# Two-bank PSUM tiles and row-tiled attention, with the modulation products moved to three other engines

## The chip, the cores and the metric

One core of one Trainium2 chip runs the whole program. The metric is the time on the device in microseconds (us), and the median of several runs is what counts. The engines are TensorE (PE; its weight loads are shown apart as PEld), VectorE (DVE), ScalarE (ACT), GpSimd (POOL) and SyncE (SP), which issues the loads.

## What is computed

The reference is one step of a two-layer trunk over 384 tokens: 128 context tokens ("prompt") and 256 latent tokens, of width 1024. Each layer has a mixer (three token mixers A, B, C and three gates from one wide input projection) and a squared-ReLU MLP. Before each of them the tokens are normalised and modulated by vectors computed from a conditioning vector, one for the context and one for the latents. Cut to what matters here:

```python
def trunk_layer(x, cond, l, w, ctx):
    mod = silu(cond) @ w_mod[l] + b_mod[l]              # 1024 x 6144, for two conds
    sh1, sc1, g1, sh2, sc2, g2 = split(mod, 6)
    h = rms_norm(x, norm1[l]) * (1 + sc1) + sh1
    x = x + g1 * mixer(h)
    h = rms_norm(x, norm2[l]) * (1 + sc2) + sh2
    return x + g2 * (square(relu(h @ w_fc1[l])) @ w_fc2[l])

# mixer: z = h @ w_in; A = gated linear attention (4 heads, low-rank decay gates alf @ w_a2_f, alb @ w_a2_b)
# B, C = softmax attention, 8 heads of 64: prompt against prompt, latents against local + context keys
#   p = softmax(q k^T / 8 + bias);  out = p v
# out = (sigmoid(ga) * A w_pa + sigmoid(gb) * B w_pb + sigmoid(gc) * C w_pc) @ w_o
```

## The kernel before

The large products run through "units": 512 KB of float32 weights are loaded into one of three `raw` buffers, ACT rounds them to float32r (`whi`), DVE takes the remainder (`wlo`, L172), and PE forms hi x hi, hi x lo and lo x hi (24 matmuls of 384 columns, named `mmf`, or 18 of 512, named `mmt`). `run` issues loads six units ahead, the cut three ahead, then the unit's matmuls; between units it advances up to three background tasks by one `yield` each. The tasks are the attention: `attn_prompt`, `attn_pair`, `gla_pre`, `gla_main`. The Tile framework then sets the order on every engine, and each engine works through its list in order.

PSUM has eight banks: four for `mmf`/`mmt`, three single-bank buffers with the tag `bx` for everything of the attention, one with the tag `md`. In `attn_pair` a pair of heads is handled in two tiles t of 128 latents. For each, two tiles `ps` (one bank a head) take the scores of 384 keys (L706), and a DVE instruction adds the mask and finds the maximum (L711). These products are plain float32 with 64 rows of contraction: one head lies in rows 0 to 63, the other in rows 64 to 127. The trace counts two passes for each float32 product. `attn_prompt` treats the two halves of the heads one after the other. `gla_pre` multiplies the gates' low-rank part with `wa2` in four products `pz` (L761) that hold only 32 rows.

The modulation vectors are made in blocks of 512 columns, each in four units of two channel blocks. Of layer 0, blocks 0 to 3 are made at the start by `mod_first`. Blocks 4 to 6 use `mod_pe`: 8 products with `sT` into four column tiles of one bank (L212). The other 17 use `mod_dve`: DVE multiplies and adds in SBUF for both conditions (L243, L245), and at the end PE transposes eight 128x128 pieces into `md` (L252), which DVE reduces (L253). `weave` puts the units between the others at places that the constants give: in layer 0's mixer `mod_pe` from unit 6 and `mod_dve` from unit 28, in layer 1's mixer `mod_dve` from unit 30, the rest in the MLPs. In the mixers these units use the same three `raw` buffers as the weights.

Of the kernel before, what the change touches and what calls it, by code (L numbers as in the profile page):

```python
# [42 lines left out]
def trunk_kernel(ctx: ExitStack, tc: tile.TileContext, A: dict):  # L43
# [8 lines left out]
    pbx = ctx.enter_context(tc.tile_pool(name="pbx", bufs=3, space=PSUM))  # L52
    pmd = ctx.enter_context(tc.tile_pool(name="pmd", bufs=1, space=PSUM))
# [54 lines left out]
    ones = pers.tile([128, 256], F32, name="ones")  # L108
# [92 lines left out]
    def mod_pe(l, cc, acc_alloc, raw_alloc=None):  # L201
        w = A["w_mod"][l].rearrange("(k p) n -> p k n", p=128)
        out = []
        for u in range(4):
# [20 lines left out]
            out.append(un)
        return out

    def mod_dve(l, cc, alloc, raw_alloc=None):
        """512 adaLN columns: products summed over the channel blocks on the vector engine, over the partitions by PE."""
        w = A["w_mod"][l].rearrange("(k p) n -> p k n", p=128)  # L230
        out = []
        for u in range(4):
            def comp(un, u=u):
# [3 lines left out]
                for i in range(2):  # L237
                    kt = 2 * u + i
                    wv = un.raw[:, i * 512:(i + 1) * 512]
                    for c in range(2):  # L240
                        s_ = sT[:, kt, c:c + 1]
                        if kt == 0:
                            ts(acc[c], wv, s_, ALU.mult)  # L243
                        else:
                            stt(acc[c], wv, s_, acc[c], ALU.mult, ALU.add)  # L245
                if u == 3:
                    c4 = slice(4 * cc, 4 * cc + 4)
                    m = modcol[l][:, c4, :]
                    for c in range(2):
                        pc = pmd.tile([128, 4, 128], F32, tag="md", name="md")  # L250
                        for i in range(4):
                            nc.tensor.transpose(pc[:, i, :], acc[c][:, i * 128:(i + 1) * 128], ident)  # L252
                        nc.vector.tensor_reduce(out=m[:, :, c], in_=pc, axis=AX.X, op=ALU.add)  # L253
                    tt(m, m, last(P(f"bm{l}")[:, c4], 2), ALU.add)
# [251 lines left out]

# [869 lines left out]
```

## Time and profile before

| | |
|---|---|
| median of 3 runs (lowest, highest) | 1435.33 us (1434.57, 1438.09) |
| profiled execution, its own span | 1433.7 us, 24064 instructions |
| PE busy | 1406.7 us (98%), 9386 matmul passes |
| PEld busy | 1274.5 us (89%) |
| DVE busy | 1008.5 us (70%) |
| ACT busy | 694.5 us (48%) |
| POOL busy | 29.5 us (2%) |
| granted TensorE clock, mean | 0.999 |

Busy time of an engine is the union of its instructions' spans. A matmul's span ends when its results have landed, so the spans of neighbours overlap, and a PE that waits for less than such a tail does not look idle. The pitch of PE is read from the starts of neighbouring matmuls instead. The profiled execution spans 1.6 us less than the median of the runs.

### The profile page before, as it was taken

Reading aid. Unit: us, or ns where it says so; the run is one execution under the profiler, and the core shown is the slowest. Engines: PE = TensorE matmul, PEld = TensorE weight load, DVE = VectorE, ACT = ScalarE, POOL = GpSimd, SP = SyncE. Lnnn points to the kernel's source line nnn. Section 1 sums busy time; section 2 is a strip of 40 time slices with the busy share of each in tenths; the row PEclk is TensorE's granted clock in tenths of the full one; section 3 lists DMA queues with packets and bytes.
Section 4 is the critical chain, followed back from the end, with each engine's and each line's share of the span. In section 5 each row is a group of like instructions: output and inputs, shape, how many; then the busy total and the mean of one; then the engine's idle time right before and its main releaser. Section 6 shows DMA issues by size and latency. Waiting matters only on the chain.

```text
span 1433.7 us, 24064 instructions
## 1 busy us (share of the span) xinstructions
PE 1406.7 (98%) x9386; PEld 1274.5 (89%) x9386; DVE 1008.5 (70%) x2032; ACT 694.5 (48%) x1260; POOL 29.5 (2%) x55
## 2 busy tenths in 40 slices
PE   6999999999999999999999999999999999999998
PEld 5876667889999999999998677689999999999998
DVE  5577466977767888877777875779986688553332
ACT  3456357643335666633335565565433556663221
POOL 0000000010000000000000000000200000000000
PEclk9999999999999999999999999999999999999999
DMA  9842533464654556556654325434555465343441
GB/s 282 232 128 79 149 99 96 134 184 135 173 177 148 179 183 183 178 193 195 191 159 125 89 59 141 127 96 112 171 155 176 147 194 159 118 130 121 137 141 61
DMA packets 191762, 212.70 MB, mean 148 GB/s; under 512 B 22656, under 2 KB 152832, under 8 KB 191648
## 3 DMA queue, kind: packets, MB, share of 16 engines
q1 hardware_dynamic: 189760, 206.18, 49.1%
q0 software_dynamic: 1600, 4.59, 0.8%
q8 instruction: 74, 1.21, 0.4%
q14 instruction: 40, 0.33, 0.1%
q10 hardware_dynamic: 288, 0.39, 0.1%
HBM read 206.15 MB, written 4.98 MB: 147 GB/s over the span
## 4 chain that ended last, share of the span: by engine, by line
PE 81%; DVE 10%; DMA 3%; ACT 2%; issue 2%; SPq 0%; DVEq 0%; ACTq 0%
PE mmf L76 57%; PE mmt L76 13%; DVE wlo L64 3%; PE ps L76 3%; PE po L76 2%; DMA raw<-in_w_in_dram 2%; PE pp L732 2%; DVE macc L67 1%; PE md L76 1%; ACT whi L57 1%; PE md L252 1%; DVE dd L64 1%; DMA raw<-in_w_mod_dram 1%; DVE K L64 1%; DVE Q L64 1%
## 5 line engine op out<-in xcount | busy, mean ns | idle before, releaser
L64 DVE TENSOR_TENSOR wlo<-raw,whi 128x1024 fp32r<-128x1024 f32 (+1 forms) x280 | 338.9, 1210 | 216.9 <-ACT whi L57 216.0
L57 ACT ACTIVATE whi<-raw 128x1024 fp32r<-128x1024 f32 (+1 forms) x280 | 293.9, 1050 | 389.7 <-PE mmf L76 283.0
L76 PE MATMUL mmf<-hh,whi 128*128 128x386 f32 (+1 forms) x960 | 328.3, 344 | 0.5 <-ACT whi L57 0.5
L76 PE MATMUL mmf<-hh,wlo 128*128 128x386 f32 (+1 forms) x960 | 327.0, 341 | 0.0
L76 PE MATMUL mmf<-hl,whi 128*128 128x386 f32 (+1 forms) x960 | 326.7, 340 | 0.0
L76 PEld LDWEIGHTS mmf<-hh,whi 128*128 128x128 f32 x960 | 181.1, 189 | 7.5 <-issue 5.4
L76 PEld LDWEIGHTS mmf<-hl,whi 128*128 128x128 f32 x960 | 181.6, 189 | 1.1 <-issue 0.9
L76 PEld LDWEIGHTS mmf<-hh,wlo 128*128 128x128 f32 x960 | 181.5, 189 | 0.5 <-DVE wlo L64 0.2
L76 PE MATMUL mmf<-h2h,wlo 128*128 128x384 f32 x512 | 173.7, 339 | 0.0
L76 PE MATMUL mmf<-h2h,whi 128*128 128x384 f32 x512 | 173.7, 339 | 0.0
L76 PE MATMUL mmf<-h2l,whi 128*128 128x384 f32 x512 | 173.4, 339 | 0.0
L76 PE MATMUL mmt<-whi,hh 128*128 128x512 f32 (+1 forms) x336 | 131.2, 392 | 0.0
L76 PE MATMUL mmt<-wlo,hh 128*128 128x512 f32 (+1 forms) x336 | 130.5, 388 | 0.0
L76 PE MATMUL mmt<-whi,hl 128*128 128x512 f32 (+1 forms) x336 | 129.0, 384 | 0.0
L67 DVE SCALAR_TENSOR_TENSOR macc<-mraw,sT,macc 128x512 f32<-128x512 f32 x140 | 99.1, 749 | 5.2 <-DMA mraw<-in_w_mod_dram 5.2
L76 PEld LDWEIGHTS mmf<-h2h,whi 128*128 128x128 f32 x512 | 96.1, 188 | 0.0
L76 PEld LDWEIGHTS mmf<-h2l,whi 128*128 128x128 f32 x512 | 96.1, 188 | 0.0
L76 PEld LDWEIGHTS mmf<-h2h,wlo 128*128 128x128 f32 x512 | 96.1, 188 | 0.0
L57 ACT ACTIVATE rl<-rl,sw 128x128 f32<-128x128 f32 (+1 forms) x128 | 51.5, 447 | 60.7 <-DVE rl L64 60.5
L76 PEld LDWEIGHTS mmt<-whi,hh 128*128 128x128 f32 x336 | 63.1, 188 | 19.6 <-issue 7.9
L67 DVE SCALAR_TENSOR_TENSOR macc<-raw,sT,macc 128x512 f32<-128x512 f32 x98 | 70.2, 753 | 10.9 <-DMA raw<-in_w_mod_dram 10.9
L76 PEld LDWEIGHTS mmt<-wlo,hh 128*128 128x128 f32 x336 | 63.3, 188 | 15.3 <-issue 5.6
(248 smaller groups left out, 2002.3 us busy)
## 6 DMA issues: line engine op xcount, KB each, us to landing
raw<-in_w_fc_dram SPq DMA_DIRECT2D x128, 512.0 KB, 3.6
raw<-in_w_in_dram SPq DMA_DIRECT2D x96, 512.0 KB, 3.8
mraw<-in_w_mod_dram SPq DMA_DIRECT2D x56, 512.0 KB, 4.7
raw<-in_w_mod_dram SPq DMA_DIRECT2D x40, 512.0 KB, 3.9
raw<-in_w_o_dram SPq DMA_DIRECT2D x16, 512.0 KB, 3.5
raw<-in_w_in_dram SPq DMA_DIRECT2D x24, 256.0 KB, 5.0
raw<-in_w_pb_dram SPq DMA_DIRECT2D x16, 256.0 KB, 4.3
raw<-in_w_pc_dram SPq DMA_DIRECT2D x8, 512.0 KB, 3.5
```

What stands on the lines that cost most here:

```text
L57: return nc.scalar.activation(out=out, in_=in_, func=func, **kw)
L64: nc.vector.tensor_tensor(out=out, in0=a, in1=b, op=op)
L67: nc.vector.scalar_tensor_tensor(out=out, in0=a, scalar=s, in1=b, op0=op0, op1=op1)
L76: nc.tensor.matmul(out, lhsT, rhs, start=start, stop=stop)
L252: nc.tensor.transpose(pc[:, i, :], acc[c][:, i * 128:(i + 1) * 128], ident)
L732: nc.tensor.transpose(pp[:, s, :], sc[:, t, c * 128:(c + 1) * 128], ident)
```

## The change

PSUM: the three `bx` buffers and the `md` buffer become two buffers of two banks each (`bx2`); single-bank users take the first bank of one. Scores: the two heads' products alternate in pieces of 256 and 128 columns, each head in a bank of its own; a `yield` stands after each t, and a pair of mixer C starts when the pair before it has its scores. Prompt: all eight heads in one pass of the task, with the two halves' last products alternating. Gates: `al` is repeated four times so that the four `pz` products lie in four row tiles of 32. Modulation: both `mod_pe` and `mod_dve` give way to `mod_units`: the context's sums stay on DVE, the latents' products go to ACT (in place, in the loaded buffer) and their sums to POOL; at the end DVE transposes 32x32 blocks and reduces, and PE sums over partitions with a 128x32 matrix `fold`, four products of 8 columns. Layer 0's mixer then weaves all of blocks 4 to 9 from unit 5, every 1.7 units; layer 1's mixer blocks 6 to 9 from unit 12, every 2.2.

```diff
-    pbx = ctx.enter_context(tc.tile_pool(name="pbx", bufs=3, space=PSUM))
-    pmd = ctx.enter_context(tc.tile_pool(name="pmd", bufs=1, space=PSUM))
+    pbx = ctx.enter_context(tc.tile_pool(name="pbx", bufs=2, space=PSUM))
...
+    def bx2(name):
+        return pbx.tile([128, 2, 512], F32, tag="bx", name=name)
+
+    def bank(t, b, shape):
+        n = int(np.prod(shape[1:]))
+        v = t[0:shape[0], b, 0:n]
+        return v if len(shape) == 2 else v.rearrange("p (a b) -> p a b", b=shape[2])
+
+    def bx(shape, name):
+        return bank(bx2(name), 0, shape)
...
+    fold = pers.tile([128, 32], F32, name="fold")
+    nc.vector.tensor_reduce(out=fold, in_=ident.rearrange("p (b i) -> p i b", i=32), axis=AX.X, op=ALU.add)
...
-    def mod_pe(l, cc, acc_alloc, raw_alloc=None):
...
-    def mod_dve(l, cc, alloc, raw_alloc=None):
+    def mod_units(l, cc, alloc, tmp, raw_alloc=None):
...
                     wv = un.raw[:, i * 512:(i + 1) * 512]
+                    if kt == 0:
+                        ts(acc[0], wv, sT[:, 0, 0:1], ALU.mult)
+                        act(acc[1], wv, AF.Copy, scale=sT[:, 0, 1:2])
+                    else:
+                        stt(acc[0], wv, sT[:, kt, 0:1], acc[0], ALU.mult, ALU.add)
+                        act(wv, wv, AF.Copy, scale=sT[:, kt, 1:2])
+                        nc.gpsimd.tensor_tensor(out=acc[1], in0=wv, in1=acc[1], op=ALU.add)
+                if u == 3:
+                    part = small.tile([128, 32], F32, tag="part", name="part", bufs=2)
                     for c in range(2):
...
+                        tr = tmp()
+                        nc.vector.transpose(tr, acc[c])
+                        nc.vector.tensor_reduce(out=part[:, 16 * c:16 * c + 16], in_=tr.rearrange("p (b j) -> p b j", j=32),
+                                                axis=AX.X, op=ALU.add)
+                    pv = part.rearrange("p (c q a) -> p a q c", c=2, a=4)
+                    ps = bx([128, 4, 2], "md")
+                    for a in range(4):
+                        mm(ps[32 * a:32 * a + 32], fold, pv[:, a])
...
-                ps = [bx([128, T], "ps") for _ in range(2)]
+                ps = bx2("ps")
                 o = 256 - 128 * t
-                for r, p_ in zip(rows, ps):
-                    mm(p_, qT[r, j, 128 + 128 * t:256 + 128 * t], M["kTB"][r, 128:512] if m == "B" else M["kTC"][r, j, o:o + T])
+                for c0, n in ((0, 256), (256, 128)):
+                    for i, r in enumerate(rows):
+                        kk = M["kTB"][r, 128 + c0:128 + c0 + n] if m == "B" else M["kTC"][r, j, o + c0:o + c0 + n]
+                        mm(ps[:, i, c0:c0 + n], qT[r, j, 128 + 128 * t:256 + 128 * t], kk)
...
+            po = bx([128, 4, 128], "po")
+            for j in range(4):
+                for half, r in halves:
                     v = M["vB"][:, 0, r] if m == "B" else M["vC"][:, 0, (2 * j + half) * 64:(2 * j + half) * 64 + 64]
-                    mm(po[r, j, :], v, pT[:, j, :])
+                    mm(po[r, j, :], v, pTs[half][:, j * 128:(j + 1) * 128])
...
+            pz = [bx2("pz") for _ in range(2)]
+            for c0, n in ((0, 256), (256, 128)):
+                for i in range(4):
+                    r = slice(32 * i, 32 * i + 32)
+                    mm(pz[i // 2][:, i % 2, c0:c0 + n], wa2[r, :], alT[r, c0:c0 + n])
...
-MOD0, MODE0, MOD1, MODE1, MOD2, MODE2, MODS, MODM = 6, 2.5, 30, 2, 28, 2.4, 2, 2
+MOD0, MODE0, MOD1, MODE1, MODS, MODM = 5, 1.7, 12, 2.2, 2, 2
```

The first place is PE in layer 0's mixer where the scores of B's first three pairs stand (`ps`; `mmt` are the input projection's matmuls). Before:

```order
L76 MATMUL mmt_1215<-wlo_1011,hh_273 128x512
L76 MATMUL ps_1137<-kTB_105,qTB_107 128x384
L76 MATMUL ps_1138<-kTB_105,qTB_107 128x384
L76 MATMUL ps_1143<-kTB_105,qTB_107 128x384
L76 MATMUL ps_1144<-kTB_105,qTB_107 128x384
L76 MATMUL ps_1179<-kTB_105,qTB_107 128x384
L76 MATMUL ps_1180<-kTB_105,qTB_107 128x384
L76 MATMUL ps_1185<-kTB_105,qTB_107 128x384
L76 MATMUL ps_1186<-kTB_105,qTB_107 128x384
L76 MATMUL ps_1196<-kTB_105,qTB_107 128x384
L76 MATMUL ps_1197<-kTB_105,qTB_107 128x384
L76 MATMUL ps_1202<-kTB_105,qTB_107 128x384
```

On the same engine at the same place in the changed program:

```order
L75 MATMUL mmt_1257<-whi_1043,hh_272 128x512
L75 MATMUL ps_1121<-kTB_104,qTB_106 128x256 x2
L75 MATMUL ps_1121<-kTB_104,qTB_106 128x128 x2
L75 MATMUL ps_1132<-kTB_104,qTB_106 128x256 x2
L75 MATMUL ps_1132<-kTB_104,qTB_106 128x128 x2
L75 MATMUL mmt_1257<-wlo_1044,hh_272 128x512
L75 MATMUL mmt_1257<-whi_1043,hl_273 128x512
L75 MATMUL ps_1157<-kTB_104,qTB_106 128x256 x2
L75 MATMUL ps_1157<-kTB_104,qTB_106 128x128 x2
L75 MATMUL ps_1164<-kTB_104,qTB_106 128x256 x2
L75 MATMUL ps_1164<-kTB_104,qTB_106 128x128 x2
L75 MATMUL mmt_1243<-whi_1239,hh_272 128x512
```

Eleven scores in a row, each in a buffer of its own, have become groups of two buffers, two heads in each, with projection matmuls between them.

The second place is PE, also in layer 0's mixer, where a unit of the modulation stands (`md`). Before, one unit of `mod_pe`:

```order
L76 MATMUL mmt_1229<-whi_1010,hh_273 128x512
L76 MATMUL mmt_1229<-wlo_1011,hh_273 128x512
L76 MATMUL mmt_1229<-whi_1010,hl_274 128x512
L76 MATMUL md_1014<-raw_932,sT_85 32x512 x2
L76 MATMUL mmt_1215<-whi_1211,hh_273 128x512
L76 MATMUL mmt_1215<-wlo_1212,hh_273 128x512
```

In the changed program PE has only the end of a block, on the same engine and in the same stage:

```order
L75 MATMUL mmt_1593<-whi_1378,hl_273 128x512
L75 MATMUL mmt_1579<-whi_1547,hl_273 128x512
L622 MATMUL pq_1517<-ident_77,cq_1155 128x128 x4
L75 MATMUL md_1564<-part_1557,fold_84 32x8 x4
L75 MATMUL mmt_1586<-whi_1547,hh_272 128x512
L75 MATMUL mmt_1586<-wlo_1548,hh_272 128x512
```

Twelve units of two products of 512 columns and their transposes are gone there; four products of 8 columns stand once a block.

The third place is DVE early in layer 0's MLP, at the end of a modulation block (`rl`, `sw`, `h2l` belong to the MLP's activations). Before:

```order
L64 TENSOR_TENSOR rl_5161<-mmf_5103,nrb_4832 128x384
L64 TENSOR_TENSOR wlo_5173<-raw_5084,whi_5172 128x1024
L64 TENSOR_TENSOR h2l_4943<-rl_5140,h2h_4942 128x384
L64 TENSOR_TENSOR h2l_4943<-rl_5161,h2h_4942 128x384
L253 TENSOR_REDUCE modcol0_91<-md_5208 128x4
L64 TENSOR_TENSOR wlo_5224<-raw_5122,whi_5223 128x1024
L253 TENSOR_REDUCE modcol0_91<-md_5214 128x4
L71 TENSOR_SCALAR macc_5303<-mraw_5116,sT_85 128x512
L64 TENSOR_TENSOR modcol0_91<-modcol0_91,par_78 128x8
```

Changed, DVE at the same block's end (`macc_4957` is the sum that POOL adds up):

```order
L66 SCALAR_TENSOR_TENSOR macc_4956<-mraw_5063,sT_82,macc_4956 128x512 x2
L63 TENSOR_TENSOR wlo_4966<-raw_4894,whi_4965 128x1024
L1177 COPY sw_4978<-mmf_4866 128x2
L63 TENSOR_TENSOR rl_4977<-mmf_4866,nrb_4864 128x384
L1177 COPY sw_4993<-mmf_4873 128x2
L63 TENSOR_TENSOR rl_4992<-mmf_4873,nrb_4864 128x384
L1177 COPY sw_5008<-mmf_4880 128x2
L238 STREAM_TRANSPOSE mtr_5248<-macc_4956 128x512
L238 STREAM_TRANSPOSE mtr_5251<-macc_4957 128x512
L1177 COPY sw_5023<-mmf_4887 128x2
L239 TENSOR_REDUCE part_5247<-mtr_5248 128x16
L63 TENSOR_TENSOR h2l_4976<-rl_4977,h2h_4975 128x384
```

Where DVE took a finished transpose out of PSUM, it now transposes itself, and its second transpose reads what POOL has written.

## Rows read from the trace of the kernel before

**Rows 1.** The page's first part: busy us (share of the span) xinstructions.
```profile
PE 1406.7 (98%) x9386; PEld 1274.5 (89%) x9386; DVE 1008.5 (70%) x2032; ACT 694.5 (48%) x1260; POOL 29.5 (2%) x55
```

**Rows 2.** Windows: length, then PE, PEld, DVE, ACT, POOL busy, PEclk, DMA, GB/s.
```profile
75.00:350.00 275.00, 271.03 (x2117) 208.31 (x2116) 205.67 (x482) 149.74 (x313) 8.71 (x16) 0.99 0.45 125
465.00:758.00 293.00, 293.00 (x1687) 290.96 (x1686) 229.12 (x411) 138.54 (x229) 4.40 (x8) 1.00 0.59 180
830.00:1065.00 235.00, 230.84 (x1955) 190.75 (x1954) 191.06 (x403) 125.58 (x248) 9.60 (x14) 1.00 0.45 124
```

**Rows 3.** Instruction groups by form on PE: xcount | busy us, mean ns.
```profile
L76 PE MATMUL ps<-kTC,qTC 64*128 64x384 f32 x64 | 23.1, 533 | 0.7 <-ACT pT L57 0.7
...
L252 PE MATMUL md<-ident,macc 128*128 128x128 f32 x136 | 21.4, 280 | 0.6 <-DVE modcol L253 0.5
L76 PE MATMUL ps<-kTB,qTB 64*128 64x384 f32 x64 | 19.7, 535 | 0.2
L76 PE MATMUL md<-raw,sT 128*32 128x512 f32 x48 | 14.7, 605 | 0.0
...
L76 PE MATMUL pz<-alT,wa 32*128 32x384 f32 x16 | 7.0, 527 | 0.0
...
L76 PE MATMUL po<-pT,vB 128*64 128x128 f32 x32 | 4.4, 279 | 0.0
```

**Rows 4.** Timeline in layer 0's scores of B: start us, length us, engine, instruction.
```profile
104.65 6.45 PE L76 MATMUL ps<-kTB,qTB 64*128 64x384 f32 x22
...
106.67 0.61 DVE L711 CUSTOM_DVE_ANT_0 sc<-ps,swam,par 128x384 f32<-128x384 f32 x1
...
106.81 0.29 PEld L76 LDWEIGHTS ps<-kTB,qTB 64*128 64x128 f32 x2 [0.24 <-DVE mx L711]
```

**Rows 5.** Timeline of PE: products of two column tiles, then of two row tiles.
```profile
123.93 1.51 PE L76 MATMUL po<-pT,vB 128*64 128x256 f32 x12
...
163.12 1.16 PE L76 MATMUL sp<-kTC,qTC 64*128 64x128 f32 x16
```

**Rows 6.** Timeline of PE around one unit of the old PE modulation.
```profile
116.68 0.40 PE L76 MATMUL mmt<-wlo,hh 128*128 128x512 f32 x1
116.91 0.40 PE L76 MATMUL mmt<-whi,hl 128*128 128x512 f32 x1
117.23 1.05 PE L76 MATMUL md<-raw,sT 128*32 128x512 f32 x4
118.22 0.50 PE L76 MATMUL mmt<-whi,hh 128*128 128x512 f32 x1
118.55 0.39 PE L76 MATMUL mmt<-wlo,hh 128*128 128x512 f32 x1
```

**Rows 7.** Timeline of PE in layer 0's MLP, at the transposes of a block.
```profile
532.71 0.60 PE L252 MATMUL md<-ident,macc 128*128 128x128 f32 x4
533.06 0.42 PE L76 MATMUL mmf<-hh,whi 128*128 128x386 f32 x1
533.32 0.33 PE L76 MATMUL mmf<-hl,whi 128*128 128x386 f32 x1
533.49 0.34 PE L76 MATMUL mmf<-hh,wlo 128*128 128x386 f32 x1
```

**Rows 8.** Instruction groups by form on DVE and ACT: xcount | busy us, mean ns.
```profile
L67 DVE SCALAR_TENSOR_TENSOR macc<-mraw,sT,macc 128x512 f32<-128x512 f32 x140 | 99.1, 749 | 5.2 <-DMA mraw<-in_w_mod_dram 5.2
...
L253 DVE TENSOR_REDUCE modcol<-md 128x4 f32<-128x512 f32 x34 | 23.4, 687 | 18.1 <-PE md L252 18.1
...
L57 ACT ACTIVATE macc<-md 128x512 f32<-128x512 f32 x3 | 1.8, 601 | 6.0 <-PE md L76 6.0
```

**Rows 9.** POOL's groups by form, and its copies by tile (duration ns min/median/max).
```profile
L131 POOL MEMSET tb<- 128x640 f32 x2 | 1.2, 634 | 0.0
...
L828 POOL COPY As<-Ac x16: 334/696/1450, 287.8 to 1011.9; 32x192 f32<-32x192 f32 x16
```

**Rows 10.** DVE's sums by tile (min/median/max ns), while POOL copied at 1007 to 1011.
```profile
L67 DVE SCALAR_TENSOR_TENSOR macc<-raw,sT,macc x4: 824/826/852, 1007.5 to 1009.7; 128x512 f32<-128x512 f32 x4
```

More of the change, by code (lines that the diff above doesn't have):

```diff
@@ L239, in comp @@
                     wv = un.raw[:, i * 512:(i + 1) * 512]
-                    for c in range(2):
[L241 to L246, printed above, removed]
-                    c4 = slice(4 * cc, 4 * cc + 4)
[L248 to L254, printed above, removed]
+                    if kt == 0:
[7 more added lines that the diff above has]
+                    part = small.tile([128, 32], F32, tag="part", name="part", bufs=2)
+                    for c in range(2):
+                        tr = tmp()
[6 more added lines that the diff above has]
+                        mm(ps[32 * a:32 * a + 32], fold, pv[:, a])
+                    c4 = slice(4 * cc, 4 * cc + 4)
+                    tt(modcol[l][:, c4, :], ps, last(P(f"bm{l}")[:, c4], 2), ALU.add)
                     mod_done(l, cc)
@@ L505, in w25 @@
             return mt([128, 640], "w25", 4, name)
-        def bx(shape, name):
-            return pbx.tile(shape, F32, tag="bx", name=name)
         M["vB"] = mt([128, 4, 128], "vB", 1, "vB")
@@ new lines, in attn_prompt @@
+                    mm(sp[:, half, j * 128:(j + 1) * 128], qT[r, j, 0:128], kk)
+            s8 = sp.rearrange("p h (j k) -> p (h j) k", k=128)
+            mx = small.tile([128, 16], F32, tag="mx", name="mx", bufs=2)
+            nc.vector.tensor_reduce(out=mx[:, 0:8], in_=s8, axis=AX.X, op=ALU.max)
+            sk = P(f"sink{l}")
+            if m == "B":
+                tt(mx[:, 0:8], mx[:, 0:8], sk, ALU.max)
+            ts(mx[:, 8:16], mx[:, 0:8], -1.0, ALU.mult)
+            dn = small.tile([128, 16], F32, tag="dn", name="dn", bufs=2)
@@ new lines, in attn_prompt @@
+            prs = [t2("pr").rearrange("p (j k) -> p j k", j=4) for _ in range(2)]
+            for i in range(8):
+                act(prs[i // 4][:, i % 4, :], s8[:, i, :], AF.Exp, bias=mx[:, 8 + i:9 + i], accum_out=dn[:, i:i + 1])
+            if m == "B":
+                tt(dn[:, 8:16], sk, mx[:, 0:8], ALU.subtract)
+                act(dn[:, 8:16], dn[:, 8:16], AF.Exp)
+                tt(dn[:, 0:8], dn[:, 0:8], dn[:, 8:16], ALU.add)
+            yield
+            nc.vector.reciprocal(dn[:, 0:8], dn[:, 0:8])
@@ new lines, in attn_prompt @@
+            for half, r in halves:
+                tt(prs[half], prs[half], last(dn[:, 4 * half:4 * half + 4], 128), ALU.mult)
+            yield
+            pp = bx2("pp")
+            for i in range(8):
+                nc.tensor.transpose(pp[:, i // 4, (i % 4) * 128:(i % 4 + 1) * 128], prs[i // 4][:, i % 4, :], ident)
+            pTs = [t2("pT") for _ in range(2)]
+            for half, r in halves:
+                act(pTs[half], pp[:, half, :])
+            yield
+            po = bx([128, 4, 128], "po")
@@ L710, in attn_pair @@
                                    (consts["tb"][i][:, o:o + T], -3.0e38))
-                    nc.vector.tensor_tensor_reduce(out=scs[i][:, t, 0:T], in0=ps[i], in1=bias, scale=1.0, scalar=floor,
+                    nc.vector.tensor_tensor_reduce(out=scs[i][:, t, 0:T], in0=ps[:, i, 0:T], in1=bias, scale=1.0, scalar=floor,
                                                    op0=ALU.add, op1=ALU.max, accum_out=mxs[i][:, t:t + 1])
-            for half, (r, h, sc, mx) in enumerate(zip(rows, heads, scs, mxs)):
+                if t == 1:
+                    done.add(N(f"sc{m}{j}"))
+                yield
+            for h, sc, mx in zip(heads, scs, mxs):
                 dn = small.tile([128, 2], F32, tag="dn2", name="dn2")
-                yield
                 n = T
@@ L802, in products @@
                 s = t if s is None else s
-                ps = [bx([128, 2, 128], "pA") for _ in range(2)]
+                pa = bx2("pA")
+                ps = [bank(pa, hp, [128, 2, 128]) for hp in range(2)]
                 for g in range(2):
@@ L813, in blocks @@
             def blocks(Q, K, w, x):
-                ps = [bx([128, 6, w], "pA") for _ in range(2)]
+                pa = bx2("pA")
+                ps = [bank(pa, hp, [128, 6, w]) for hp in range(2)]
                 for i in range(6):
@@ L1009, in ev_cv @@
                 for j in range(4):
[L1010 removed]
+                    spawn(N(f"aC{j}"), after([N(f"ck{i}") for i in range(3)] + [N(f"scC{i}") for i in range(j)], attn_pair("C", j)))
                 spawn(N("gpre"), after([N("aBp")] + [N(f"aB{j}") for j in range(4)], gla_pre()))
@@ L1032, in comp @@
                             fps[c] = pmm.tile([128, T], F32, tag="mm", name="mmf")
+                        two = bx2("mmt")
                         for t in range(3):
-                            fps[4 + t] = bx([128, 512], "mmt")
+                            fps[4 + t] = two[:, t, :] if t < 2 else mdst["pair"][:, 0, :]
                     hh, hl = hs["hh"][:, kt, :T], hs["hl"][:, kt, :T]
```

147 lines of the change are left out of this document (48 added, 99 removed).

## Prediction

> **What bounds the kernel now.** I read the page's first part, then the windows of the stages, then single stretches of PE. PE is busy for 1406.7 of 1433.7 us [rows 1], and in layer 0's MLP, 465 to 758 us, for every one of 293 us [rows 2]; there the reader is to see that nothing but fewer PE passes can help. In the mixers PE is nearly as busy (271.0 of 275 us, 230.8 of 235), but DVE stands at 205.7 and 191.1 us [rows 2]. And PE's busy time hides waits there. In the stretch with B's scores 22 passes take 6.45 us of "busy", and the weight load in the middle of it shows why: it waits for `mx`, which DVE writes when it empties a score bank, at 0.61 us an instruction [rows 4]. Three banks of `bx` hold three scores; from then on PE gets one bank at a time, 6.45 / 11 = 0.59 us a score (two passes each), and the two heads, which could run side by side, run one after the other. So the bound is PE's list: its passes, plus waits that look like passes. The granted clock is 1.00 or 0.99 in these windows (2.4 GHz) [rows 2]; I expect no change of it.
>
> **What the change takes from PE, part by part.** Times are pitches, from the start of a group to the start of what follows, since busy spans overlap.
>
> Scores. There are 32 pairs of scores (2 layers, 2 mixers, 4 pairs, 2 tiles t), 128 passes, 23.1 + 19.7 = 42.8 us busy [rows 3]. Side by side, 12 passes of 256 columns in two tiles of the array are six steps in 1.51 us, 0.25 us a step; 16 passes of 128 columns in two row tiles are eight steps in 1.16 us, 0.145 us a step [rows 5]. A step of these holds its part of the last one's tail, which I leave in for entering and leaving another tile shape: from the `mmt` at 116.91 to `md` are 0.32 us, and from the first `mmt` behind it to the next 0.33, where two neighbouring `mmt` are 0.23 apart [rows 6], 0.2 us a visit. A new pair is two steps of each, 2 x 0.25 + 2 x 0.145 = 0.79 us, and 32 of them 25.3 us: a gain of 17.5. Bounds: if DVE still sets the pace, 64 emptyings at 0.59 are 37.8 us and the gain is 5; it ends at 20 if the visits vanish too. I take 16, because two buffers hold two whole pairs and the order puts projection matmuls behind each two, which leaves DVE time.
>
> The Trainium skill speaks to this in "TensorEngine Tiling (Array Packing)", Performance Considerations: tiling speeds up the products, not the emptying of PSUM, which can become the limit. The trace agrees [rows 4], with 0.59 us a bank by DVE; by it alone the scores' gain would be the 5 above.
>
> Modulation. A unit of `mod_pe` stands from 117.23 to 118.22, 0.99 us, with 0.09 us more ahead and 0.10 behind [rows 6]: 1.18 x 12 units = 14.2 us, and the transposes of its three blocks like a group below, 3 x 0.43 = 1.3. In `mod_dve` four transposes take 0.35 us, and the following matmul is 0.26 from the next instead of 0.17 [rows 7]: 0.43 a group, 34 groups, 14.6 us. Together 30.1 us leave. What comes is `fold` in 20 blocks: eight passes over 8 columns, four column tiles, two after another. No row has it. Below: nothing but the visit, 0.2 us. Above: eight steps of 0.145 us one by one and the visit, 1.4 us. I take two steps and a half and the visit, 0.5 us, near to the side-by-side row: 10 us. Net gain 20, between 2 and 26.
>
> Gates. 16 passes `pz`, 7.0 us [rows 3], become, for each of the two layers, two steps of 256 and two of 128 columns over four tiles at once, 0.79 and a visit: gain 5. Prompt. The products with v, 4.4 us for B [rows 3] and as much for C, become eight steps of 0.145 in each of four places, 4.6: gain 4. The probabilities' transposes stand in sixes instead of threes, 32 groups fewer at 0.08: gain 2. Sum for PE: 16 + 20 + 5 + 4 + 2 = 47 us.
>
> **What it gives to the others.** DVE loses seven of eight second sums: a block was 14 sums of 0.749, two first products and two reduces of 0.687 [rows 8], about 12.8 us; it is now seven sums, one product, two transposes and two reduces. The transposes' price is bounded by nothing and by 1.2 us (twice a reduce of the same 512 columns); at 0.6 each the block is 8.3 us. ACT gets eight products of 0.6 us a block [rows 8], 96 us on 694.5; in the mixers it has room (149.7 of 275). POOL gets seven adds a block, 140 in all. From below an add costs what a memset of 640 columns suggests, 0.634 x 512 / 640 = 0.51 us; from above what a copy of 192 columns suggests twice over, 0.334 x 512 / 192 x 2 = 1.8 us [rows 9]. I take 1.06, two operands each at the memset's pace. The skill's "GPSIMD Engine Reference", section 3, gives 4497 ns for an add of 2048 columns; as an estimate from that page 1.1 us for 512.
>
> The price of this lies in the mixers, because POOL and DVE hold each other up. While POOL copied at 1007 to 1011 us, DVE's sums took 824 to 852 ns instead of 749 [rows 8, 10], and POOL's copies took 696 ns in the middle, up to 1450, where 334 is the least [rows 9]. Layer 0's mixer, 75 to 350 us: PE's share of the gain is about 8 of the scores, 15 of the modulation (all of `mod_pe`), and 4.5 of the rest, so 275 becomes 248. DVE had 205.7; the window gains six blocks (50 us) and loses about two blocks' worth of the old `mod_dve` units (26 us): 230. POOL's 42 adds there are 44 us. If DVE were stopped for all of them it would need 274 and PE's gain would be lost; if for none, 230 and nothing is lost. I take half, 252 against PE's 248, and with queueing between two engines so close a charge of 10. Layer 1's mixer, 830 to 1065: PE 235 - 15 = 220; DVE 191 - 18 = 173, with all 28 adds 203, still below: charge 2. In the MLPs DVE has 229 of 293 us [rows 2] and loses 36 in layer 0's; nothing.
>
> Other edits cost nothing I can see: the repeated `al` is one DVE copy a layer, hidden under PE's projection matmuls and 0.5 us if that cover is gone; loads keep their number and size, and a modulation unit holds its `raw` buffer while DVE, ACT and POOL pass over it (about 0.75 + 0.6 + 2 x 1.06), as long as four DVE sums held it before (4 x 0.749).
>
> **Sum.** 47 - 12 = 35 us off 1433.7 is 1399. The runs' median lies 1.6 us above this span: 1400 us.
>
> **Rivals.** First, DVE and POOL bind both mixers. The skill's "SBUF — State Buffer", Who interferes with whom, calls the ports that VectorE shares with GpSimd an exclusive lock: a DVE instruction with two SBUF inputs and a GpSimd instruction that reads SBUF block each other fully. The lengths above agree in direction. With every add felt, layer 0's mixer keeps its 275 us (27 lost) and layer 1 gives back half of its 15: 47 - 35 = 12 off, 1423 us. Against it: emptyings from PSUM take one operand from there, and much of the DVE list is of that kind.
>
> Second, nothing of POOL is felt: 47 off, 1388, or 1380 where small waits of the mixers shrink too. For it: in rows 10 a sum lost only 0.08 us to a copy. Third, the scores stay at DVE's pace and `fold` at half its way to the poor end (gains 5 and 11): 47 - 11 - 9 - 12 = 15 off, 1420 us.
>
> Fourth, slower. One block's end is now a chain over four in-order queues: DVE's sum, ACT's product in the same buffer, POOL's add, DVE's second transpose, and `fold` on PE. ACT and DVE can stand still at the head of their queues while emptyings and weight cuts wait behind. If each of 20 blocks stops PE for more than 47 / 20 = 2.35 us, the change loses; at 3.5 us it ends at 1433.7 + 70 - 47 + 1.6 = 1458 us. For it: in layer 0's MLP DVE's second transpose stands just eight rows behind its last sums, and a copy could take 1450 ns [rows 9]. Against it: in that MLP, DVE will be idle a third of the time (193 of 293 us), and `fold` stands far behind in PE's list.
>
> **How the numbers follow.** Chances: my forecast, 1388 to 1412, 0.52; the second rival 0.13; the first and third together, 1412 to 1430, 0.21; no gain or loss to speak of 0.05; slower 0.09. The range leaves out the slow case and the far end of the second: 1382 to 1428. Runs before spread over 3.5 us, so 0.3% (4.3 us) is about what can be told from no change. Faster by more than that: 0.52 + 0.13 + 0.21 = 0.86; within 0.05; slower 0.09.
>
> **What would show it.** Right: the score stretch of B shorter than 5 us for its first six pairs, with two starts a few ns apart in each step; no `md<-raw`; `fold` groups of about 0.3 us; PE still at 97% or more; DVE down by some 50 us, ACT near 790, POOL's adds near 1.06 us alone and longer beside DVE. Wrong: PE idle or stretched matmuls before `fold` in the MLPs (fourth rival), `wlo` and `macc` of 1.5 us or more and PE waiting for `wlo` in 100 to 300 us (first), single scores still at DVE's pace (third).

## The result and the profile after

The changed kernel takes 1476.89 us (median of 4 runs, 1474.72 to 1477.62) where the kernel before took 1436.10 in the same comparison: a ratio of 1.0285, with a 95% interval of 1.0271 to 1.0299. It is slower by 2.9%; the forecast was 1400 us. The profiled execution has a span of 1475.2 us.

The page's first part, which answers [rows 1]:

```profile
PE 1387.3 (94%) x9494; PEld 1278.6 (87%) x9494; DVE 1037.7 (70%) x1944; ACT 779.2 (53%) x1377; POOL 255.2 (17%) x195
```

PE has lost 19 us of busy time and yet stands idle for 87.9 us of the span (27.0 before). DVE, which lost work, is busy for 29 us more.

Four windows of the stages, with the columns of [rows 2] (layer 0's mixer, the first and second part of its MLP, layer 1's mixer):

```profile
80.00:320.00 240.00, 216.72 (x1911) 172.83 (x1910) 206.59 (x429) 150.63 (x304) 62.02 (x47) 0.96 0.43 122
474.00:623.00 149.00, 136.79 (x775) 132.84 (x774) 128.66 (x195) 103.48 (x191) 55.27 (x35) 0.99 0.59 183
623.00:763.00 140.00, 140.00 (x818) 138.91 (x817) 86.62 (x115) 63.76 (x89) 40.95 (x27) 1.00 0.54 170
800.00:1050.00 250.00, 228.14 (x2016) 187.08 (x2015) 206.09 (x429) 155.01 (x312) 50.55 (x44) 0.98 0.43 122
```

PE now waits in both mixers and, against the forecast, in the first part of the MLP; it has no wait in the second part, though POOL works there for 41 us. The granted clock, 0.99 to 1.00 in [rows 2], has fallen to 0.96 in the first window.

Instruction groups by form (columns as in [rows 3] and [rows 8]):

```profile
L63 DVE TENSOR_TENSOR wlo<-raw,whi 128x1024 fp32r<-128x1024 f32 x272 | 350.4, 1289 | 255.7 <-ACT whi L56 254.5
L233 POOL TENSOR_TENSOR macc<-mraw,macc 128x512 f32<-128x512 f32 x70 | 114.9, 1641 | 369.7 <-ACT mraw L56 335.7 <-DVE h2l L63 23.9 <-issue 5.5
L233 POOL TENSOR_TENSOR macc<-raw,macc 128x512 f32<-128x512 f32 x70 | 112.3, 1604 | 476.6 <-ACT raw L56 332.1 <-ACT al L56 74.1 <-PE mmt L75 42.3
L66 DVE SCALAR_TENSOR_TENSOR macc<-mraw,sT,macc 128x512 f32<-128x512 f32 x70 | 67.4, 962 | 22.6 <-DMA mraw<-in_w_mod_dram 21.6
L238 DVE STREAM_TRANSPOSE mtr<-macc 128x512 f32<-128x512 f32 x40 | 27.2, 696 | 2.3 <-POOL macc L233 2.3
...
L75 PE MATMUL md<-part,fold 128*32 128x8 f32 x160 | 5.0, 186 | 3.7 <-DVE part L239 3.3 <-ACT pT L56 0.3
```

An add on POOL lasts 1.60 to 1.64 us instead of the 1.06 assumed. A sum on DVE lasts 0.962 us in the MLPs, where [rows 8] had 0.749. The `fold` of a block is 5.0 / 20 = 0.25 us, and DVE waits for POOL before its second transpose for only 2.3 us in all.

What PE waits for, over the whole run (us in total, times, longest us):

```profile
PE mmf L75 <- DVE wlo L63: 15.5, 13, 3.0
...
PE poT L962 <- DVE on L63: 7.1, 3, 4.0
PE mmf L75 <- ACT whi L56: 5.9, 6, 2.2
PE pq L592 <- DVE bo L63: 5.7, 2, 3.4
PE pA L75 <- DVE K L63: 5.3, 4, 1.8
```

Of the 15.5 us for `wlo`, 8.7 lie in the first part of layer 0's MLP and only 2.9 in layer 0's mixer. In both mixers PE mostly waits for results of the token mixers that DVE owes it (`on`, `bo`, `K`).

Two of PE's waits in that MLP. The first, from the timeline of 581.45 to 588 us:

```profile
581.26 4.59 POOL L233 TENSOR_TENSOR macc<-mraw,macc 128x512 f32<-128x512 f32 x3 [7.31 <-ACT mraw L56]
...
581.47 1.67 DVE L66 SCALAR_TENSOR_TENSOR macc<-mraw,sT,macc 128x512 f32<-128x512 f32 x1
...
583.07 1.65 DVE L63 TENSOR_TENSOR h2l<-rl,h2h 128x384 fp32r<-128x384 f32 x1
...
584.64 2.29 DVE L63 TENSOR_TENSOR wlo<-raw,whi 128x1024 fp32r<-128x1024 f32 x1
...
586.98 0.45 PE L75 MATMUL mmf<-hh,wlo 128*128 128x386 f32 x1 [1.91 <-DVE wlo L63]
```

Beside three adds, three DVE instructions in a row take 1.67, 1.65 and 2.29 us. With both sums on DVE (first experiment) their kinds take 0.74, 0.55 and 1.22 in the mean, so the three lose 3.1 us together. DVE has no pause between them, and PE stands still for 1.91 us until `wlo` is there.

The second, from the timelines of 533 to 546 us:

```profile
534.85 0.37 SPq L174 DMA_DIRECT2D mraw<-in_w_mod_dram  x1
...
539.21 0.75 DVE L66 SCALAR_TENSOR_TENSOR macc<-mraw,sT,macc 128x512 f32<-128x512 f32 x1 [3.31 <-DMA mraw<-in_w_mod_dram]
539.88 1.22 DVE L63 TENSOR_TENSOR wlo<-raw,whi 128x1024 fp32r<-128x1024 f32 x1
...
541.15 0.69 PE L75 MATMUL mmf<-hh,wlo 128*128 128x386 f32 x1 [2.29 <-DVE wlo L63]
...
541.64 0.53 PE L75 MATMUL mmf<-hh,whi 128*128 128x386 f32 x1
...
541.96 0.53 PE L75 MATMUL mmf<-hl,whi 128*128 128x386 f32 x1
```

This one came about in another way. `wlo` itself has its usual 1.22 us, but DVE stood for 3.31 us before the sum ahead of it, for a load of `mraw`. SyncE issued that load at 534.85, just after POOL's add of 532.84 to 534.82 us had set the buffer free. Of the seven waits of PE for `wlo` in the MLP's first part (8.7 us) this is the one with such a pause shortly before it; in the nine microseconds ahead of the other six no pause of DVE is longer than 0.42 us.

Behind this wait PE's matmuls start 0.32 us apart. The windows of single microseconds show why (columns as above):

```profile
540.00:541.00 1.00, 0.00 (x0) 0.00 (x0) 1.00 (x1) 0.95 (x2) 0.10 (x1) 1.00 0.92 353
541.00:542.00 1.00, 0.85 (x3) 0.85 (x4) 1.00 (x2) 0.97 (x3) 1.00 (x1) 0.53 0.09 33
542.00:543.00 1.00, 1.00 (x5) 1.00 (x4) 1.00 (x2) 0.68 (x1) 0.23 (x1) 0.50 0.65 138
543.00:544.00 1.00, 1.00 (x5) 1.00 (x4) 1.00 (x3) 0.66 (x1) 0.00 (x0) 0.50 1.03 354
544.00:545.00 1.00, 1.00 (x6) 1.00 (x5) 1.00 (x2) 0.54 (x2) 0.79 (x1) 0.76 0.10 32
545.00:546.00 1.00, 1.00 (x8) 1.00 (x7) 1.00 (x1) 0.25 (x1) 0.92 (x2) 1.00 0.00 0
...
587.00:588.00 1.00, 1.00 (x6) 1.00 (x7) 1.00 (x2) 0.50 (x2) 0.00 (x0) 1.00 0.71 170
```

PE had stood still for 2.3 us, and then the granted clock is 0.50 (1.2 GHz) for some 3.4 us: five matmuls a microsecond instead of eight. Behind the wait of 1.91 us at 586.98 the clock stays at 1.00, so not every wait has this sequel.

### The profile page after: what moved, and what is told of

It is laid out like the page before. It is cut to its first block, busy times and chain, and to the rows that moved or that the text cites. A ratio compares the mean times of both kernels' runs of the same rounds, so it can differ in the third digit from the quotient of the medians.

```text
span 1475.2 us, 24675 instructions
## 1 busy us (share of the span) xinstructions
PE 1387.3 (94%) x9494; PEld 1278.6 (87%) x9494; DVE 1037.7 (70%) x1944; ACT 779.2 (53%) x1377; POOL 255.2 (17%) x195
## 3 DMA queue, kind: packets, MB, share of 16 engines
q8 instruction: 75, 1.23, 0.3%
## 4 chain that ended last, share of the span: by engine, by line
PE 54%; DVE 14%; DMA 4%; ACT 4%; issue 3%; POOL 1%; DVEq 0%; SPq 0%; POOLq 0%; ACTq 0%
PE mmf L75 46%; DVE wlo L63 4%; PE mmt L75 3%; DVE macc L66 2%; DMA mraw<-in_w_mod_dram 2%; DMA raw<-in_w_in_dram 1%; PE poA L75 1%; DMA raw<-in_w_mod_dram 1%; POOL macc L233 1%; ACT whi L56 1%; PE po L75 1%; ACT rl L56 1%; DVE dd L63 1%; DVE sc L703 1%; PE pp L728 1%
## 5 line engine op out<-in xcount | busy, mean ns | idle before, releaser
L63 DVE TENSOR_TENSOR wlo<-raw,whi 128x1024 fp32r<-128x1024 f32 (+1 forms) x280 | 356.4, 1274 | 261.9 <-ACT whi L56 260.7
L75 PE MATMUL mmf<-hh,wlo 128*128 128x386 f32 (+1 forms) x960 | 330.6, 345 | 14.4 <-DVE wlo L63 14.4
L75 PE MATMUL mmf<-hh,whi 128*128 128x386 f32 (+1 forms) x960 | 331.7, 347 | 4.7 <-ACT whi L56 3.4
L233 POOL TENSOR_TENSOR macc<-raw,macc 128x512 f32<-128x512 f32 x70 | 112.3, 1604 | 476.6 <-ACT raw L56 332.1
L233 POOL TENSOR_TENSOR macc<-mraw,macc 128x512 f32<-128x512 f32 x70 | 114.9, 1641 | 369.7 <-ACT mraw L56 335.7
L75 PE MATMUL mmt<-wlo,hh 128*128 128x512 f32 (+1 forms) x328 | 126.3, 386 | 0.0
L66 DVE SCALAR_TENSOR_TENSOR macc<-mraw,sT,macc 128x512 f32<-128x512 f32 x70 | 67.4, 962 | 22.6 <-DMA mraw<-in_w_mod_dram 21.6
```

The costliest lines, as they stand in the source:

```text
L63: nc.vector.tensor_tensor(out=out, in0=a, in1=b, op=op)
L66: nc.vector.scalar_tensor_tensor(out=out, in0=a, scalar=s, in1=b, op0=op0, op1=op1)
L233: nc.gpsimd.tensor_tensor(out=acc[1], in0=wv, in1=acc[1], op=ALU.add)
```

## The experiments

Three theories. A: POOL's adds and DVE's work on SBUF hold each other up, DVE comes late with `wlo` and other results, PE waits, and the clock falls behind some of the waits. B: the new chain DVE, ACT, POOL, DVE stands at the heads of in-order queues (the fourth rival). C: neither; the attention with two PSUM buffers, or the modulation's earlier places, cost the time. Times below are medians; the kernel before took 1435.75 to 1437.26 us beside them.

**Both sums on DVE.**

```diff
-                        act(wv, wv, AF.Copy, scale=sT[:, kt, 1:2])
-                        nc.gpsimd.tensor_tensor(out=acc[1], in0=wv, in1=acc[1], op=ALU.add)
+                        stt(acc[1], wv, sT[:, kt, 1:2], acc[1], ALU.mult, ALU.add)
```

> The changed kernel with the second sum of the modulation back on DVE: 140 DVE sums more (0.75 us each alone, 105 us), no ACT product in place, no POOL add. Theory A (POOL's adds of 1.6 us and DVE's two-operand instructions hold each other up, DVE's wlo comes late, PE waits): DVE's sums go back from 0.96 to about 0.75 us and wlo from 1.27 to 1.21 us, PE's stall goes, 1395 to 1420 us. Theory B (the chain over DVE, ACT, POOL and DVE again waits at the heads of in-order queues): the chain is gone too, so the same 1395 to 1420. Theory C (not the engines of the modulation, but the new attention with two PSUM buffers, or the modulation's earlier places, cost the time): 1460 us or more, since DVE has even more to do.

1414.85 us, ratio 0.9851 (0.9832 to 0.9869). C falls: with attention, `fold` and places as in the changed kernel the time is 62 us lower. DVE is busier than in the changed kernel, 1054.5 us against 1037.7, and still PE waits less (idle for 45.8 us, not 87.9): the sum of DVE's busy time is not what counts. Its groups:

```profile
L63 DVE TENSOR_TENSOR wlo<-raw,whi 128x1024 fp32r<-128x1024 f32 x272 | 332.1, 1221 | 222.6 <-ACT whi L56 220.6
...
L66 DVE SCALAR_TENSOR_TENSOR macc<-mraw,sT,macc 128x512 f32<-128x512 f32 x140 | 99.0, 744 | 3.6 <-DMA mraw<-in_w_mod_dram 3.6
...
L63 DVE TENSOR_TENSOR h2l<-rl,h2h 128x384 fp32r<-128x384 f32 x64 | 35.2, 551 | 7.0 <-ACT h2h L56 6.5
```

**The kernel before with the new modulation alone** (`mod_units`, `fold`, the new places and the one-column `ones` in the kernel before; attention and PSUM as they were).

> The kernel before with the new modulation alone (engines, fold and places of the changed kernel; old attention, three single-bank buffers and the md bank). Theory A and B: the loss is the modulation's and the attention's gain of about 25 to 30 us on PE is missing too: 1490 to 1515 us. Theory C: the modulation's passes that leave PE are a gain and nothing else follows: 1410 to 1430 us.

1500.09 us, ratio 1.0439 (1.0411 to 1.0466). The loss comes from the modulation; the attention's part of the change is worth 1500.1 - 1476.9 = 23 us beside it (the four runs of this kernel spread over 8 us).

**No adds on POOL.** The line with `nc.gpsimd.tensor_tensor` is taken out.

> The changed kernel without POOL's adds (seven of the eight terms of the latents' sum are left out of the modulation; ACT's products in place stay, DVE's second transpose reads the first product). Theory A: DVE's sums at 0.75 us, 1385 to 1410 us. Theory B with its weight on DVE waiting for POOL: also 1385 to 1410; with its weight on ACT waiting at the head of its queue for DVE's sum: ACT's waits of some 67 us stay and so does most of the loss, 1440 us or more. Theory C: 1465 us or more.

1401.52 us, ratio 0.9762 (0.9746 to 0.9777). So 140 adds cost 75 us. ACT still scales in place behind DVE's sums and waits for them (16 and 25 us in two groups), and DVE still waits 25.9 us for the load of `mraw`; with these waits in it PE is idle for 36.8 us, not 87.9. The page:

```profile
PE 1364.4 (97%) x9494; PEld 1262.9 (90%) x9494; DVE 963.0 (69%) x1944; ACT 777.4 (55%) x1377; POOL 28.7 (2%) x55
```

and the mean granted clock of this kernel, then of the changed one:

```profile
core 0: 1401.2 us, clock 0.999
```

```profile
core 0: 1475.2 us, clock 0.984
```

The 74.0 us between the two spans can be counted: PE is idle 87.9 instead of 36.8 us, 51.1 more, and a mean clock of 0.984 instead of 0.999 is 23.6 - 1.4 = 22.2 us of full speed lost. Together 73.3. The clock's part shows once more in PE's busy time, which is 22.9 us longer for the same 9494 passes. By windows of one microsecond most of it lies in the mixers (14 us from 75 to 350, 7 from 763 to 1070), 1.7 in layer 0's MLP.

**Adds whose result nobody needs.**

```diff
-                        nc.gpsimd.tensor_tensor(out=acc[1], in0=wv, in1=acc[1], op=ALU.add)
+                        nc.gpsimd.tensor_tensor(out=wv, in0=wv, in1=wv, op=ALU.add)
```

> The changed kernel with POOL's adds of the same size and number in the same places, but adding each product to itself in the loaded buffer (the latents' sum keeps only its first term): POOL works as long on SBUF, but DVE's second transpose no longer waits for POOL. Theory A: the adds hold DVE up as before, 1460 to 1480 us, DVE's sums still about 0.95 us. Theory B (DVE waits for POOL at the end of a block): 1390 to 1415 us.

1451.96 us, ratio 1.0115 (1.0096 to 1.0134): in neither theory's range. 50 of the 75 us are there without the chain's end. The other 25 were open, for these adds are also shorter: the shortest takes 1.03 us, the shortest of the changed kernel 1.27.

**The same adds behind both sums on DVE** (the last line of the diff above, added to the first experiment's kernel; no instruction of DVE or ACT reads what POOL writes, and only the loaded buffer comes free later).

> The kernel with both sums on DVE (1414.85 us) and 140 POOL adds beside it that nothing needs: each adds a loaded piece of 128x512 to itself after DVE's sums have read it. No instruction of DVE or ACT waits for POOL; only the loaded buffer comes free later. Theory A (POOL's and DVE's work on SBUF hold each other up): 1450 to 1490 us, DVE's sums above 0.80 us where they were 0.745, and more PE time at half the granted clock behind waits for wlo. Theory B (the chain's waits at the heads of queues cost the time): 1413 to 1422 us.

1462.93 us, ratio 1.0189 (1.0172 to 1.0206): 48 us more than without them, as A says and a chain of results cannot. DVE's group:

```profile
L66 DVE SCALAR_TENSOR_TENSOR macc<-mraw,sT,macc 128x512 f32<-128x512 f32 x140 | 130.5, 968 | 1.2 <-DMA mraw<-in_w_mod_dram 1.0
```

A sum takes 0.968 instead of 0.744 us, with no wait for a load, and DVE's busy time rises from 1054.5 to 1125.3.

**No wait of DVE for POOL.**

```diff
-                        nc.vector.transpose(tr, acc[c])
+                        nc.vector.transpose(tr, acc[0])
```

> The changed kernel with DVE's second transpose reading DVE's own sum instead of POOL's (the latents' modulation vectors are wrong by that; POOL's adds stay as they are). Adds in place cost 50 us and the sums of the changed kernel 75 us over no adds at all, so 25 us lie open. If DVE's wait for POOL at a block's end is what they are: 1450 to 1458 us. If they are the adds' own length (1.62 us in the changed kernel, 1.39 in place): 1470 to 1477 us.

1479.25 us, ratio 1.0310 (1.0295 to 1.0326): no gain. B falls at this place. That the 25 us go with the adds' length is then the reading left, and the next run tests length.

**Half the columns.** The add takes `[:, 0:256]` of its operands.

> The changed kernel with POOL's adds over 256 of the 512 columns (seven terms of the latents' sum are left out in the other half); the number of adds, the waits and their order stay. Theory A: the loss goes with POOL's busy time, half of 75 us above the 1401.5 without adds, 1430 to 1448 us. Theory B: the waits stay as many, and the loss nearly too, 1460 to 1475 us.

1435.82 us, ratio 1.0004 (0.9992 to 1.0017): 34 us above no adds, against 75 for whole adds. With as many adds and waits the loss is less than half; a half add lasts 1.02 us in the mean.

One way of B is left, that of the wait at 541 us: an add keeps its loaded buffer, the next load starts later, and DVE stands before a sum until it lands. Over the run DVE's sums wait so for 31.2 us in the changed kernel, 32.6 without adds, 36.6 with half adds, 12.9 with the adds behind both sums and 10.7 with both sums alone. The times, in this order 1476.9, 1401.5, 1435.8, 1462.9 and 1414.9 us, do not follow them. So these waits do not make the loss by themselves; what they add to single stalls was not measured apart.

**Side by side.** Behind the last output of the first experiment's kernel, groups of free instructions:

```diff
+        pool = lambda: nc.gpsimd.tensor_tensor(out=P1[:, h], in0=P0[:, h], in1=P1[:, h], op=ALU.add)
+        dstt = lambda: stt(V1[:, h], V0[:, h], sT[:, 0, 0:1], V1[:, h], ALU.mult, ALU.add)
+        dtt = lambda: tt(V1, V0, V1, ALU.subtract)
+        dts = lambda: ts(V1[:, h], V0[:, h], 0.5, ALU.mult)
+        dps = lambda: tt(V1[:, h], ps, V0[:, h], ALU.subtract)
+        sc = lambda: act(C0[:, h], C0[:, h], AF.Copy, scale=sT[:, 0, 1:2])
```

> The kernel with both sums on DVE, and behind its last output some 120 us of instructions that need nothing of each other, group by group: POOL's adds of 128x512 alone, DVE's sums alone, both side by side, then the same with DVE's 1024-column difference (as wlo), with a one-operand scale, with a difference that reads PSUM, POOL's copy beside DVE's sum, POOL's add beside ACT's scale, DVE's sum beside ACT's scale. Theory A: side by side with POOL's add a DVE sum grows from 0.745 us to 1.0 us or more and the add from about 1.1 to 1.4 us or more, so that the pair takes nearly the sum of both; the instructions with one SBUF operand, and ACT's, keep their time. Theory B: the lengths change by less than 10%. The whole time, some 1530 us, says nothing here.

Its instructions by tile (ns shortest/median/longest), DVE's first: `va` is DVE's tile and `vps` a PSUM bank. The shortest is the time alone, the longest the time beside a POOL add.

```profile
L66 DVE SCALAR_TENSOR_TENSOR va<-va,sT,va x30: 742/752/1634, 1420.1 to 1510.8; 128x512 f32<-128x512 f32 x30
L70 DVE TENSOR_SCALAR va<-va x16: 418/427/1369, 1458.9 to 1471.5; 128x512 f32<-128x512 f32 x16
L63 DVE TENSOR_TENSOR va<-vps,va x16: 679/691/692, 1472.3 to 1488.5; 128x512 f32<-128x512 f32 x16
...
L63 DVE TENSOR_TENSOR va<-va,va x11: 1215/1226/2166, 1438.0 to 1457.3; 128x1024 f32<-128x1024 f32 x11
```

POOL's adds by stretch, one answer each: alone, beside DVE's sums, beside the 1024-column difference, beside the one-operand scale, beside the difference that reads PSUM.

```profile
L1295 POOL TENSOR_TENSOR pa<-pa,pa x4: 1257/1262/1266, 1414.3 to 1418.3; 128x512 f32<-128x512 f32 x4
...
L1295 POOL TENSOR_TENSOR pa<-pa,pa x3: 1589/1589/1698, 1421.1 to 1424.5; 128x512 f32<-128x512 f32 x3
...
L1295 POOL TENSOR_TENSOR pa<-pa,pa x3: 2121/2122/2169, 1439.4 to 1443.9; 128x512 f32<-128x512 f32 x3
...
L1295 POOL TENSOR_TENSOR pa<-pa,pa x6: 1322/1323/1373, 1459.5 to 1466.6; 128x512 f32<-128x512 f32 x6
...
L1295 POOL TENSOR_TENSOR pa<-pa,pa x5: 1262/1262/1262, 1473.2 to 1478.5; 128x512 f32<-128x512 f32 x5
```

Side by side a DVE sum takes 1.63 instead of 0.75 us, a `wlo`-like difference 2.17 instead of 1.23, a scale 1.37 instead of 0.43: each loses 0.88 to 0.94 us to the add that it meets. Only the difference with an operand in PSUM keeps its time, and the add beside it too. ACT's scale keeps its 0.72 us. A was right but for the one-operand scale, which was expected to be spared. The Trainium skill says this in "SBUF — State Buffer", Who interferes with whom: GpSimd shares a port pair with VectorE under an exclusive lock, and VectorE needs it for a second SBUF input and for the two-port modes that scales can enter. The trace agrees in which kinds are held. It does not show the lock held for the whole of an add: beside the sums an add starts every 1.67 us, where 1.26 + 0.75 would be 2.01.

**POOL in the MLPs only** (the mixers' ten blocks with both sums on DVE).

> The changed kernel with the second sums of the mixers' ten blocks on DVE; only the ten blocks of the MLPs keep ACT's products in place and POOL's adds. With both sums on DVE everywhere the time is 1414.85 us, with POOL everywhere 1476.9. The prediction's step (the MLPs feel nothing, the mixers everything): 1412 to 1417 us. If an add costs DVE its time wherever DVE is at its limit for a while, as the first part of an MLP seems to be: 1425 to 1440 us, with waits of PE for wlo between 475 and 600 us.

1435.68 us, ratio 0.9989 (0.9978 to 1.0000): of the 62 us between both sums on DVE and the changed kernel, POOL in the MLPs alone brings 21, where the prediction had nothing. Windows of 475 to 600 us, in this kernel and, second, with both sums on DVE:

```profile
475.00:600.00 125.00, 116.65 (x659) 113.33 (x658) 107.19 (x156) 91.22 (x169) 44.75 (x28) 0.99 0.57 179
```

```profile
475.00:600.00 125.00, 125.00 (x731) 123.92 (x730) 114.39 (x198) 78.42 (x142) 0.00 (x0) 1.00 0.63 192
```

PE finishes 659 passes instead of 731 in the same time. DVE's 156 instructions are no measure beside 198, for its list is shorter here: the second sums are gone from it. It is busy for less of the stretch, 107 instead of 114 us, and PE waits all the same.

**Other places, both sums on DVE.** Three runs change only the constants of the first experiment's kernel: wider spread in both mixers; two blocks moved from layer 1's mixer to layer 0's MLP; the moved blocks with the wider spread in layer 0's mixer, and in layer 1's, instead of the spread, a later start (unit 24). The first of them:

```diff
-MOD0, MODE0, MOD1, MODE1, MODS, MODM = 5, 1.7, 12, 2.2, 2, 2
+MOD0, MODE0, MOD1, MODE1, MODS, MODM = 5, 2.0, 12, 2.8, 2, 2
```

> The kernel with both sums on DVE, the modulation's units in the mixers spread wider (every 2.0 instead of 1.7 units in layer 0, every 2.8 instead of 2.2 in layer 1). Its 13 us above the kernel without adds (1401.5) are DVE's load in the mixers; if the load's peak is what makes wlo late, a wider spread gives 1406 to 1412 us; if it is the sum over the mixer, 1413 to 1417.

1404.90 us, ratio 0.9773 (0.9759 to 0.9788): better than either kernel, and 3.4 us above no adds at all. It is 1 us under the range for a peak of load as the cause.

> The kernel with both sums on DVE, two blocks of layer 1 made in layer 0's MLP instead of layer 1's mixer (units there every 1.7 instead of 2). DVE has room in that MLP and none in the mixer: 1405 to 1411 us. If the MLP's first part is already at DVE's limit, no gain: 1414 to 1420 us.

1410.17 us, ratio 0.9815 (0.9797 to 0.9833): 4.7 us gained.

> The two edits of places together, and the last two blocks of layer 1's mixer from unit 24. If DVE's peaks are the cause: 1402 to 1408 us; if not, 1413 to 1418 us.

1410.47 us, ratio 0.9814 (0.9799 to 0.9828): in neither range, and 5.6 us above the spread alone. Between 465 and 763 us DVE is busy for 263.8 us here and for 242.1 in the spread kernel, and PE is idle for 2.3 us where it was for none; between 763 and 1070 us PE is idle for 9.5 instead of 6.7 us. So the moved blocks cost where they went; which of the two edits in layer 1's mixer does the rest was not tested.

## Why the prediction was wrong

**What leaves PE: right.** Busy time of single tiles over the run: scores 42.8 to 28.9 us (13.9 gained, 16 forecast), `pz` 7.0 to 3.4 (3.6, 5), `po` 35.7 to 32.7 (3.0, 4), `pp` 33.7 to 31.1 (2.6, 2). These make 23.1 us, near what the second experiment gives for the attention. From the kernel before to no adds PE's busy time falls by 1406.7 - 1364.4 = 42.3 us, so 19 are the modulation's (20 forecast). The sum of 47 came out as 42. Even without adds the time is 35 us lower and not 42, because PE is idle for 36.8 us there, 10 more than in the kernel before. A tile of scores now takes 0.92 us for its eight passes:

```profile
112.76 1.58 PE L75 MATMUL ps<-kTB,qTB 64*128 64x256 f32 x16
115.35 0.92 PE L75 MATMUL ps<-kTB,qTB 64*128 64x256 f32 x8 [0.34 <-DVE mx L703]
```

**What DVE loses: right.** Without the adds DVE's busy time is 45.5 us lower (some 50 forecast), ACT's 777 us (near 790).

**The failed step: the charge of 12 us, "10 in layer 0's mixer, 2 in layer 1's, nothing in the MLPs".** The runs showed 75. Two things in it were wrong.

First, a size: an add is not 1.06 but 1.26 us alone and 1.6 beside DVE; the bounds of 0.51 and 1.8 held it. By luck this did no harm. The step took half of each add from DVE, 0.53 us, and DVE's busy time did grow by 1037.7 - 963.0 = 74.7 us, 0.53 an add.

Second, and this decided it, the step weighed DVE's total in a window against PE's (252 against 248, 229 of 293) as if idle time anywhere in the window could take the adds up. It can't. A `wlo` is due a few units after its load, and the sums come in lumps: with both sums on DVE it is busy for 106.8 us of the 110 from 474 to 584, and for 18.2 of the 40 behind them. That first stretch without adds, with both sums on DVE, and in the changed kernel (columns as above):

```profile
474.00:584.00 110.00, 110.00 (x646) 108.92 (x646) 84.17 (x150) 85.63 (x158) 0.00 (x0) 1.00 0.63 198
```

```profile
474.00:584.00 110.00, 110.00 (x641) 109.19 (x640) 106.82 (x188) 72.29 (x133) 0.00 (x0) 1.00 0.65 196
```

```profile
474.00:584.00 110.00, 101.44 (x573) 98.72 (x572) 100.03 (x152) 77.13 (x141) 47.58 (x30) 0.98 0.60 187
```

Without adds DVE has 26 us of room, and 30 adds at 0.53 are 16. By the sum they fit, and DVE's 100.0 us are just this sum; yet PE is idle for 8.6 us of the 110, and for 12 of the 149 up to 623 us. With both sums on DVE there are 3 us of room and PE is never idle. So a full DVE is not the trouble. What the trace shows ahead of such a wait is held instructions in a row, as at 581 us, with a late `wlo` behind them. In the second part, 623 to 763 us, 21 adds cost PE no idleness. POOL's adds are fewer there, and of the activations' `rl` and `h2l` DVE has 2 and 4 there instead of 30 and 28; which of the two spares PE was not tested.

Over whole runs more DVE time goes with more run time, but not one for one: 74.7 us of DVE with 75.4 us of run, 51.7 with 50.4 (adds in place), 26.5 with 34.3 (half adds), 70.8 with 48.1 (adds behind DVE's sums). The first pair agrees by chance, since 22 of its 75 us are the clock.

**A term that was missing: the clock.** "I expect no change of it" failed. Behind some of PE's waits its matmuls run at 1.2 GHz, as at 541 us, and that is 22 of the 74 us.

**The rivals.** The first had the right mechanism, DVE and POOL holding each other up; its price of 1423 us was too small, because it let the adds take back only what PE had gained in the mixers, and a PE that waits can fall below where it was. It stood on the faster side. Against it I held that PSUM operands escape; that is shown (0.69 us beside an add), but `wlo`, the sums and `h2l` read SBUF twice, and these are the three that were held at 581 us. The fourth, the slower one, had the right sign for another reason: its waits are there (DVE for POOL 2.3 us, ACT for DVE's sums 34.4 and 32.7), and taking the first away gained nothing. Not in it was the way through the loaded buffer, which one of PE's waits shows (2.29 us at 541). The second (nothing felt, 1388) has its counterpart in no adds, 1401.5. The third fell: the scores came out near the forecast, and `fold` at 0.25 us of PE's busy time a block, where 0.5 was taken.

## What to carry to other kernels

Work given to POOL is not free for DVE: price it as time taken from DVE's SBUF instructions. Then ask how late one result that PE needs can become when several instructions ahead of it are held, and do not weigh totals over a stage. When PE begins to wait, the clock can take more behind the waits: look at the granted clock there. Here the better division was to keep the sums on DVE and spread them wider: 1404.9 us, with nearly all of the gain on PE kept (1367.0 us busy, 1364.4 without adds).

## What the runs showed of the hardware

- A POOL add of two 128x512 float32 operands takes 1.26 us alone, 1.59 us beside DVE sums and 2.12 beside 1024-column differences; in the kernel, an add of a buffer to itself took 1.03 at the least. Side by side a DVE instruction that meets one loses 0.88 to 0.94 us, whether alone it takes 0.43, 0.75 or 1.23; in the kernel a `wlo` lost up to 1.09. The pair is not wholly serial: 1.26 + 0.75 is 2.01, and a pair took some 1.7 us.
- A one-operand scale in SBUF (0.43 us alone) is held just so, 1.37 us. A two-operand DVE instruction with one operand in PSUM kept its 0.69 us, and the add beside it 1.26. A POOL copy of 128x512 takes 0.61 us alone and up to 0.95 beside DVE's sums, which then take 0.98.
- ACT's products in place (0.72 us) and DVE's sums (0.75 us) beside them left each other's times alone, and ACT's products kept theirs beside POOL's adds too.
